# Interleaving conv blocks with the pairs of heads, respreading the adaLN steps, and fixing VectorE's order in a one-core decoder block

## The chip, the core and the metric

The kernel runs on one core of one Trainium2 chip. The metric is the device time of one execution in microseconds (us). Before the change the median of three timed runs is 1939.71 us (1936.22 to 1939.85). The core's engines each work through a queue of their own: TensorE (PE; its weight loads are shown as PEld), VectorE (DVE), ScalarE (ACT), GpSimd (POOL) and SyncE (SP), which issues the loads.

## What is computed

One decoder layer on 256 rows of 2048 columns in float32:

```
mod = silu(c) @ w_ada + b_ada                # six vectors: sh1 sc1 g1 sh2 sc2 g2
xn  = rmsnorm(x) * (1 + sc1) + sh1
q k v g | bg cg xc | gate logits = xn @ w_in
y_ret  = (rmsnorm_head(retention(rotary(q), rotary(k), v)) * silu(g)) @ w_ret_o
y_conv = (bg * conv3(cg * xc)) @ w_conv_o
h   = x + g1 * ((sig(ga) * y_ret + sig(gb) * y_conv) @ w_mix_o)
xn2 = rmsnorm(h) * (1 + sc2) + sh2
ff  = (silu(conv3(xn2 @ w_gate) + b) * (xn2 @ w_up)) @ w_down
out = rmsnorm(h + g2 * ff) * final_g
```

There are 8 heads of 256 columns, handled as four pairs; the feed-forward width is 5632.

## The kernel before

Every weight matrix is read once, in pieces of 256 rows by 512 columns (512 KB). To keep float32 accuracy a piece (`raw`) is split: ScalarE rounds it to `hi` (L304) and VectorE computes the rest, `lo = raw - hi` (L305). TensorE multiplies hi by both halves of the activations and lo by their high half. Activations are split the same way (`split`, L90).

The work is a list of **units**. A `Weights` unit is one such piece with its matmuls. `w_block` (L397) holds the weights stationary, eight units of 16 matmuls for 512 columns of output, and is used for q, k, the three conv inputs, gate and up; its four results are put together by a copy on ScalarE (L420) and an add on VectorE. `x_block` (L380) holds the activations stationary, 12 matmuls a unit, and is used for the other projections. An `Ada` unit (L310) has no matmuls of its own: it loads 128 rows of 1024 columns of w_ada and VectorE adds their product with silu(c) to an accumulator (L341). After 16 of them a sum over the partitions on TensorE gives shift or scale columns (`columns_of`, L350), or `broadcast` (L538) gives a gate's row on all partitions. `spread` (L506) puts Ada units evenly between the units of a stage.

The main loop (L1043) goes through the list: at step i it issues the load of unit i+9, prepares (hi, lo, or the adaLN step) unit i+2, runs the matmuls of unit i with what its block end (epilogue) needs, and then runs what was put off to this step by `after(n, ...)`: n steps of the list, Ada units counted. There are seven `raw` buffers and three each of `hi` and `lo`, and six PSUM banks for block results.

This is the order in which the source issues the instructions. The order on each engine is not that: the planner of the framework runs through the program with its own estimate of times and takes, engine by engine, the first instruction in source order that it holds to be ready. So an instruction that is ready early in the estimate stands earlier in the engine's queue than in the source. `tc.keep_in_program_order(ins)` puts an instruction behind the one traced just before it on its engine, without a wait for it to end; an instruction traced after it may still move ahead.

The stages by time are: a first stage in which v, the swish gate and the merge gates are computed while the first adaLN vectors arrive (to 399 us); the blocks of q and k of four pairs and the first three conv blocks (399 to 688); the retention output (688 to 785); the other nine conv blocks (785 to 999); the conv output (999 to 1096); the mixing projection (1096 to 1191); the second norm (`norm2`, L881), whose `normed` calls (L893) lie between the first feed-forward units; gate and up blocks 0 to 5 (to 1471), their down projection (to 1601), blocks 6 to 10 (to 1824) and theirs. The sequence `rotate` (L589), `scores`, `mix` and `turn` (L625 to L682) follows each k block by `after`. A conv input block ends in `gate_x` and `taps` (L740, L748). `gate_of` (L701) adds a bias that is loaded on its own and takes the sigmoid.

Of the 128 Ada units behind the first stage, 112 (`ada_mid`) are shift 2, scale 2, gate 1 and the first half of gate 2; 40 of them are spread over the q, k and first conv blocks, 13 over the retention output, 32 over the other conv blocks, 13 over the conv output and 14 over the mixing projection. The last 16 (`ada_ff`) are the second half of gate 2. The first half's broadcast is made in `norm2` (L888).

Of the kernel before, what the change touches and what calls it, by code (L numbers as in the profile page):

```python
# [10 lines left out]
F32 = mybir.dt.float32  # L11
# [4 lines left out]
ALU = mybir.AluOpType  # L16
# [3 lines left out]
D = 2048  # L20
# [3 lines left out]
CB = 512  # L24
# [13 lines left out]
ROT_AT = 24  # L38
DEFER_SG = 2
ROT_EARLY = 12  # L40
ADA_QK, ADA_RET, ADA_CONV, ADA_OUT = 40, 13, 32, 13
LAST_HEAD = 2
NORM_AHEAD = 4

# [2 lines left out]
def tile_trunk_block(  # L47
# [213 lines left out]
    later = []  # L261
    now = [0]

    def after(n, fn):
        later.append([now[0] + n, fn])

# [15 lines left out]
    class Weights:  # L282
# [11 lines left out]
        def prep(self):  # L294
            if self.in_big:
                both = blk8("hl", [P, 2, self.nk, CB], F32R)
                self.hi, self.lo = both[:, 0], both[:, 1]
            elif self.in_work:
                self.hi, self.lo = (
                    work.tile([P, self.nk, CB], F32R, tag="w4", name=nm(n)) for n in ("hw", "lw"))  # L300
            else:
                self.hi = wpool.tile([P, self.nk, CB], F32R, tag="hi", bufs=3, name=nm("hi"))
                self.lo = wpool.tile([P, self.nk, CB], F32R, tag="lo", bufs=3, name=nm("lo"))
            nc.scalar.copy(self.hi, self.raw)  # L304
            nc.vector.tensor_tensor(self.lo, self.raw, self.hi.bitcast(F32), op=ALU.subtract)  # L305

        def run(self):
            self.run_(self)
# [1 line left out]
    class Ada:  # L310
# [23 lines left out]
        def prep(self):  # L334
            acc = self.state["acc"]
            for k in range(self.nk):
                kt = self.k0 + k
                if kt == 0 and not self.bias:
                    nc.vector.tensor_scalar_mul(acc, self.raw[:, k], c_act[:, 0:1])
                    continue  # L340
                nc.vector.scalar_tensor_tensor(  # L341
                    acc, self.raw[:, k], c_act[:, kt:kt + 1], acc, op0=ALU.mult, op1=ALU.add
                )
            if self.k0 + self.nk == KT:
                self.done(acc)

# [191 lines left out]
    def broadcast(acc, store, half, name, bank):  # L538
        if "t" not in store:
            store["t"] = blk8(name, [P, D], F32)  # L540
        for s in range(2):
            ps = bank()
            nc.tensor.matmul(ps, lhsT=ones, rhs=acc[:, s, :], start=True, stop=True)
            c0 = (2 * half + s) * CB
            nc.scalar.copy(store["t"][:, c0:c0 + CB], ps)
# [2 lines left out]
        return lambda acc: broadcast(acc, g1b, half, "g1b", misc_bank)  # L548

    def gate2_done(half):  # L550
        if half:
            return lambda acc: broadcast(acc, g2b, 1, "g2b", misc_bank)
        return lambda acc: g2b.update(acc=acc)

    def vec_done(which, half):
        def done(acc):
# [7 lines left out]
    def ada_units(m, half, done, bias=False):  # L564
        st = {}
        c0 = m * D + half * 2 * CB
        return [Ada(kt, 1, c0, c0 + CB, CB, st, done, bias) for kt in range(KT)]
# [4 lines left out]
        ada_mid += ada_units(4, half, vec_done("scale", half))  # L572
    for half in range(2):
        ada_mid += ada_units(2, half, gate1_done(half), True)
    ada_mid += ada_units(5, 0, gate2_done(0), True)
    ada_ff = ada_units(5, 1, gate2_done(1), True)

    def take(extra, n):
        got = extra[:n]
# [191 lines left out]

    convs = [b for j in range(4) for b in conv_blocks(j)]

    seq = []
    for pair in range(4):
        st = retention(pair, {})
        seq += rot_block(pair * CB, st, "q")
        seq.append(decay_of(pair, st))
        seq += rot_block(D + pair * CB, st, "k")
    seq += convs[0] + convs[1] + convs[2]  # L780
    units += spread(seq, take(ada_mid, ADA_QK))

    seq = []
    for j in range(4):
# [1 line left out]
        seq += b[:2] + [gate_of(gate_a, 0, j)] + b[2:]  # L786
    units += spread(seq, take(ada_mid, ADA_RET))

    seq = [u for b in convs[3:] for u in b]
    units += spread(seq, take(ada_mid, ADA_CONV))  # L790

    mixed = []
# [88 lines left out]
    def norm2():  # L881
        ss = small.tile([P, 2], F32, tag="ss2", name="ss_h2")
        nc.vector.tensor_reduce(ss, ss_h, axis=mybir.AxisListType.X, op=ALU.add)
        r = rstd_of(ss, 2, D, "r_h")
        dr = w4("dr", [P, 2, P])
        for t in range(2):
            nc.vector.tensor_scalar_mul(dr[:, t, :], ident, r[:, t:t + 1])
        broadcast(g2b["acc"], g2b, 0, "g2b", acc_bank)  # L888
        turn_h(3)
        row["t"] = acc_bank()[:, 0:S]  # L890
        nc.tensor.matmul(row["t"], lhsT=ones, rhs=dr.rearrange("p t n -> p (t n)"), start=True, stop=True)
# [131 lines left out]
    for b0, b1_, final in ((0, cut, False), (cut, NB, True)):  # L1023
        seq = [u for j in range(b0, b1_) for u in ff_blocks(j)]
        if not final:
            seq = seq[:8] + spread(seq[8:], ada_ff, 8)
            for k0 in range(KT - 2, NORM_AHEAD - 1, -2):
                seq.insert((k0 - NORM_AHEAD) // 2 + 1, Call((lambda k: lambda: normed(k, k + 2))(k0)))
        units += seq
        if final:  # L1030
            units.append(Call(load_final))
        for j in range(4):
            args = (
                w_down, b0 * CB, j * CB,
                (lambda b: lambda kt: ff_t[b + kt // 4][:, kt % 4])(b0),
                4 * (b1_ - b0), down_epilogue(j, final),
            )
            units += last_block(*args, LAST_HEAD) if final and j == 3 else x_block(*args)


    n = len(units)
# [48 lines left out]
```

## Time and profile before

| | |
|---|---|
| median of three timed runs | 1939.71 us |
| the profiled execution | 1944.93 us |
| its span, first to last instruction | 1943.1 us |
| PE busy | 1876.3 us (97%) |
| PEld busy | 1582.6 us (81%) |
| DVE busy | 1380.0 us (71%) |
| ACT busy | 891.1 us (46%) |
| moved by DMA | 452.89 MB, mean 233 GB/s |
| mean granted TensorE clock | 0.992 |

Busy shares are means over stages with different limits. Matmuls are pipelined, so that the busy time of PE covers moments in which it starts nothing. [...] An idle time is put down to the instruction or transfer that came last.

### The profile page before, as it was taken

The page shows a single profiled execution, that of the slowest core. Times are in us where ns is not written, and L with a number is a line of the kernel's source. Part 1 is how long each engine was busy: PE and PEld are TensorE (multiplying, and loading weights), DVE is VectorE, ACT ScalarE, POOL GpSimd, SP SyncE. Part 2 cuts the span into 40 slices and gives each one's busy share as a digit, 9 for nine tenths or more (in the row PEclk, how much of TensorE's full clock was granted, in tenths as well). Part 3 has the DMA queues.
Part 4 walks back from the last instruction along what each step waited for, and adds up shares of the span by engine and source line. Part 5 has one row for each costly group of instructions (what it writes and reads, how often), then busy time and mean ns, then how long its engine had stood idle before and what let it go on. Part 6 is the DMA issues. An engine that isn't in the chain of part 4 may idle for free.

```text
span 1943.1 us, 25273 instructions
## 1 busy us (share of the span) xinstructions
PE 1876.3 (97%) x9543; PEld 1582.6 (81%) x9543; DVE 1380.0 (71%) x1638; ACT 891.1 (46%) x1150; POOL 21.8 (1%) x51
## 2 busy tenths in 40 slices
PE   5999999999999999999989999999999999999997
PEld 4788888878888877888778777888888888888886
DVE  6899987867688865677677766777765556666655
ACT  4643444534334543444444445555554335555543
POOL 1000000000000000000000000000000000000000
PEclk9999999999999999999999999999999999999999
DMA  8889986667777777787777885777665556666553
GB/s 300 305 278 308 319 306 188 207 220 242 235 234 246 237 250 245 263 269 248 249 241 259 290 266 153 232 230 225 218 205 194 192 192 192 188 192 207 193 193 112
DMA packets 222091, 452.89 MB, mean 233 GB/s; under 512 B 14932, under 2 KB 27536, under 8 KB 221584
## 3 DMA queue, kind: packets, MB, share of 16 engines
q1 hardware_dynamic: 220768, 448.99, 70.3%
q10 hardware_dynamic: 720, 2.10, 0.3%
q8 instruction: 75, 1.23, 0.2%
q14 instruction: 48, 0.39, 0.1%
q0 software_dynamic: 480, 0.18, 0.0%
HBM read 449.11 MB, written 2.10 MB: 232 GB/s over the span
## 4 chain that ended last, share of the span: by engine, by line
PE 81%; DMA 9%; DVE 6%; issue 3%; ACT 1%; SPq 0%; POOL 0%; DVEq 0%; POOLq 0%; ACTq 0%
PE acc L409 30%; PE acc L414 15%; PE acc L377 12%; PE acc L378 12%; PE acc L376 12%; DMA raw<-in_w_ada 7%; DVE lo L305 3%; DVE ada L341 1%; DMA ld<-in_b_gate 1%; PE misc L355 1%; PE misc L247 0%; ACT hi L304 0%; DMA raw<-in_w_mix_o 0%; DMA raw<-in_w_in 0%; DVE y_tok L660 0%
## 5 line engine op out<-in xcount | busy, mean ns | idle before, releaser
L304 ACT CAST hi<-raw 128x1024 fp32r<-128x1024 f32 (+1 forms) x601 | 622.9, 1038 | 837.1 <-PE acc L409 426.5
L305 DVE TENSOR_TENSOR lo<-raw,hi 128x1024 fp32r<-128x1024 f32 (+1 forms) x601 | 717.9, 1203 | 302.4 <-ACT hi L304 299.3
L409 PE MATMUL acc<-xn,hi 128*128 128x512 f32 x2688 | 852.0, 398 | 5.6 <-DVE u L734 2.5
L414 PEld LDWEIGHTS acc<-xn,lo 128*128 128x128 f32 x2688 | 507.1, 189 | 129.6 <-DVE lo L305 9.9
L414 PE MATMUL acc<-xn,lo 128*128 128x256 f32 x2688 | 531.3, 279 | 6.7 <-DVE lo L305 6.7
L409 PEld LDWEIGHTS acc<-xn,hi 128*128 128x128 f32 x2688 | 412.9, 190 | 8.8 <-DVE u L734 2.9
L341 DVE SCALAR_TENSOR_TENSOR ada<-raw,c_act,ada 128x1024 f32<-128x1024 f32 (+2 forms) x199 | 238.9, 1201 | 177.6 <-DMA raw<-in_w_ada 176.9
L377 PE MATMUL acc<-lo,ff_t 128*128 128x512 f32 x332 | 129.2, 389 | 0.0
L376 PE MATMUL acc<-hi,ff_t 128*128 128x512 f32 x332 | 129.2, 389 | 0.0
L378 PE MATMUL acc<-hi,ff_t 128*128 128x512 f32 x332 | 129.2, 389 | 0.0
L376 PE MATMUL acc<-hi,xn 128*128 128x512 f32 x304 | 119.0, 395 | 4.1 <-ACT xn L92 2.4
L377 PE MATMUL acc<-lo,xn 128*128 128x512 f32 x304 | 119.8, 394 | 1.1 <-DVE lo L305 1.1
L378 PE MATMUL acc<-hi,xn 128*128 128x512 f32 x304 | 119.4, 393 | 0.0
L420 ACT COPY sb<-acc 128x256 f32<-128x256 f32 x168 | 61.9, 370 | 44.4 <-PE acc L414 28.4
L378 PE MATMUL acc<-hw,xn 128*128 128x512 f32 x208 | 82.0, 394 | 0.0
L377 PE MATMUL acc<-lw,xn 128*128 128x512 f32 x208 | 81.9, 394 | 0.0
L376 PE MATMUL acc<-hw,xn 128*128 128x512 f32 x208 | 81.1, 394 | 0.0
L304 ACT CAST hw<-raw 128x1024 fp32r<-128x1024 f32 (+1 forms) x58 | 55.6, 959 | 48.4 <-DMA raw<-in_w_in 27.2
L377 PEld LDWEIGHTS acc<-lo,ff_t 128*128 128x128 f32 x332 | 62.3, 188 | 13.2 <-DVE lo L305 0.2
L376 PEld LDWEIGHTS acc<-hi,ff_t 128*128 128x128 f32 x332 | 62.3, 188 | 13.0
L378 PEld LDWEIGHTS acc<-hi,ff_t 128*128 128x128 f32 x332 | 62.3, 188 | 12.7
L376 PEld LDWEIGHTS acc<-hi,xn 128*128 128x128 f32 x304 | 57.1, 188 | 17.7 <-ACT xn L92 2.4
(195 smaller groups left out, 1762.4 us busy)
## 6 DMA issues: line engine op xcount, KB each, us to landing
raw<-in_w_in SPq DMA_DIRECT2D x272, 512.0 KB, 4.7
raw<-in_w_ada SPq DMA_DIRECT2D x160, 512.0 KB, 4.6
raw<-in_w_gate SPq DMA_DIRECT2D x88, 512.0 KB, 4.1
raw<-in_w_up SPq DMA_DIRECT2D x88, 512.0 KB, 4.1
raw<-in_w_down SPq DMA_DIRECT2D x88, 512.0 KB, 4.3
raw<-in_w_ret_o SPq DMA_DIRECT2D x32, 512.0 KB, 5.2
raw<-in_w_conv_o SPq DMA_DIRECT2D x32, 512.0 KB, 5.0
raw<-in_w_mix_o SPq DMA_DIRECT2D x32, 512.0 KB, 6.1
```

Source lines behind the costliest of these rows:

```text
L304: nc.scalar.copy(self.hi, self.raw)
L305: nc.vector.tensor_tensor(self.lo, self.raw, self.hi.bitcast(F32), op=ALU.subtract)
L341: nc.vector.scalar_tensor_tensor(acc, self.raw[:, k], c_act[:, kt:kt + 1], acc, op0=ALU.mult, op1=ALU.add)
L355: nc.tensor.matmul(ps[:, i:i + 1], lhsT=flat[:, (s0 + i) * P:(s0 + i + 1) * P], rhs=ones[:, 0:1], start=True, stop=True,)
L376: nc.tensor.matmul(ps, lhsT=xh, rhs=u.hi[:, k, :], start=k0 + k == first, stop=False)
L377: nc.tensor.matmul(ps, lhsT=xh, rhs=u.lo[:, k, :], start=False, stop=False)
L378: nc.tensor.matmul(ps, lhsT=xl, rhs=u.hi[:, k, :], start=False, stop=k0 + k == end - 1)
L409: nc.tensor.matmul(ps, lhsT=u.hi[:, k, i * P:(i + 1) * P], rhs=xt(k0 + k).rearrange("p h s -> p (h s)"), start=k0 + k == 0, stop=False,)
L414: nc.tensor.matmul(ps[:, 0:S], lhsT=u.lo[:, k, i * P:(i + 1) * P], rhs=xt(k0 + k)[:, 0, :], start=False, stop=last and k == UK - 1,)
L420: nc.scalar.copy(b, ps[:, S:2 * S])
```

## The change

Three things are changed. The q and k blocks of pairs 0 and 1 are followed by the three conv blocks of the first 512 columns, then come pairs 2 and 3 and the conv blocks of the next 512; six conv blocks are left for the later stage. The Ada units are respread: 6 in each pair of head pairs, 11 in each group of three conv blocks, 13 in the retention output, 24 in the six conv blocks, 12 in the conv output, and the 13 left in the mixing projection. All 32 units of gate 2 are now in the feed-forward part, 26 among the gate and up blocks and 6 in the second block of the first down projection, and both broadcasts are made where their last unit is prepared, not in `norm2`. From 12 units ahead of the first stage's end, each `lo` and each adaLN step is kept in program order on VectorE.

```diff
--- before.py
+++ after.py
@@ -38,7 +38,7 @@
 ROT_AT = 24
 DEFER_SG = 2
 ROT_EARLY = 12
-ADA_QK, ADA_RET, ADA_CONV, ADA_OUT = 40, 13, 32, 13
+ADA_QK, ADA_CONV0, ADA_RET, ADA_CONV, ADA_OUT = 6, 11, 13, 24, 12
 LAST_HEAD = 2
 NORM_AHEAD = 4
 
@@ -261,6 +261,9 @@
     later = []
     now = [0]
 
+    def in_order(ins):
+        return tc.keep_in_program_order(ins) if now[0] >= n_start else ins
+
     def after(n, fn):
         later.append([now[0] + n, fn])
 
@@ -302,7 +305,7 @@
                 self.hi = wpool.tile([P, self.nk, CB], F32R, tag="hi", bufs=3, name=nm("hi"))
                 self.lo = wpool.tile([P, self.nk, CB], F32R, tag="lo", bufs=3, name=nm("lo"))
             nc.scalar.copy(self.hi, self.raw)
-            nc.vector.tensor_tensor(self.lo, self.raw, self.hi.bitcast(F32), op=ALU.subtract)
+            in_order(nc.vector.tensor_tensor(self.lo, self.raw, self.hi.bitcast(F32), op=ALU.subtract))
 
         def run(self):
             self.run_(self)
@@ -338,9 +341,9 @@
                 if kt == 0 and not self.bias:
                     nc.vector.tensor_scalar_mul(acc, self.raw[:, k], c_act[:, 0:1])
                     continue
-                nc.vector.scalar_tensor_tensor(
+                in_order(nc.vector.scalar_tensor_tensor(
                     acc, self.raw[:, k], c_act[:, kt:kt + 1], acc, op0=ALU.mult, op1=ALU.add
-                )
+                ))
             if self.k0 + self.nk == KT:
                 self.done(acc)
 
@@ -548,9 +551,7 @@
         return lambda acc: broadcast(acc, g1b, half, "g1b", misc_bank)
 
     def gate2_done(half):
-        if half:
-            return lambda acc: broadcast(acc, g2b, 1, "g2b", misc_bank)
-        return lambda acc: g2b.update(acc=acc)
+        return lambda acc: broadcast(acc, g2b, half, "g2b", misc_bank)
 
     def vec_done(which, half):
         def done(acc):
@@ -572,8 +573,7 @@
         ada_mid += ada_units(4, half, vec_done("scale", half))
     for half in range(2):
         ada_mid += ada_units(2, half, gate1_done(half), True)
-    ada_mid += ada_units(5, 0, gate2_done(0), True)
-    ada_ff = ada_units(5, 1, gate2_done(1), True)
+    ada_ff = [u for half in range(2) for u in ada_units(5, half, gate2_done(half), True)]
 
     def take(extra, n):
         got = extra[:n]
@@ -771,14 +771,15 @@
 
     convs = [b for j in range(4) for b in conv_blocks(j)]
 
-    seq = []
-    for pair in range(4):
-        st = retention(pair, {})
-        seq += rot_block(pair * CB, st, "q")
-        seq.append(decay_of(pair, st))
-        seq += rot_block(D + pair * CB, st, "k")
-    seq += convs[0] + convs[1] + convs[2]
-    units += spread(seq, take(ada_mid, ADA_QK))
+    for half in range(2):
+        seq = []
+        for pair in (2 * half, 2 * half + 1):
+            st = retention(pair, {})
+            seq += rot_block(pair * CB, st, "q")
+            seq.append(decay_of(pair, st))
+            seq += rot_block(D + pair * CB, st, "k")
+        units += spread(seq, take(ada_mid, ADA_QK))
+        units += spread(sum(convs[3 * half:3 * half + 3], []), take(ada_mid, ADA_CONV0))
 
     seq = []
     for j in range(4):
@@ -786,7 +787,7 @@
         seq += b[:2] + [gate_of(gate_a, 0, j)] + b[2:]
     units += spread(seq, take(ada_mid, ADA_RET))
 
-    seq = [u for b in convs[3:] for u in b]
+    seq = sum(convs[6:], [])
     units += spread(seq, take(ada_mid, ADA_CONV))
 
     mixed = []
@@ -885,7 +886,6 @@
         dr = w4("dr", [P, 2, P])
         for t in range(2):
             nc.vector.tensor_scalar_mul(dr[:, t, :], ident, r[:, t:t + 1])
-        broadcast(g2b["acc"], g2b, 0, "g2b", acc_bank)
         turn_h(3)
         row["t"] = acc_bank()[:, 0:S]
         nc.tensor.matmul(row["t"], lhsT=ones, rhs=dr.rearrange("p t n -> p (t n)"), start=True, stop=True)
@@ -1023,7 +1023,7 @@
     for b0, b1_, final in ((0, cut, False), (cut, NB, True)):
         seq = [u for j in range(b0, b1_) for u in ff_blocks(j)]
         if not final:
-            seq = seq[:8] + spread(seq[8:], ada_ff, 8)
+            seq = seq[:8] + spread(seq[8:], take(ada_ff, 26))
             for k0 in range(KT - 2, NORM_AHEAD - 1, -2):
                 seq.insert((k0 - NORM_AHEAD) // 2 + 1, Call((lambda k: lambda: normed(k, k + 2))(k0)))
         units += seq
@@ -1035,7 +1035,8 @@
                 (lambda b: lambda kt: ff_t[b + kt // 4][:, kt % 4])(b0),
                 4 * (b1_ - b0), down_epilogue(j, final),
             )
-            units += last_block(*args, LAST_HEAD) if final and j == 3 else x_block(*args)
+            seq = last_block(*args, LAST_HEAD) if final and j == 3 else x_block(*args)
+            units += spread(seq, ada_ff, 4) if j == 1 and not final else seq
 
 
     n = len(units)
```

## Rows read from the trace of the kernel before

**Rows 1.** Windows: busy us and count of each engine, PE clock, DMA share, GB/s.
```profile
398.70:688.20 289.50, 280.45 (x1585) 243.55 (x1584) 220.83 (x273) 126.99 (x190) 4.11 (x5) 0.98 0.73 237
688.20:784.50 96.30, 90.36 (x402) 73.50 (x401) 60.61 (x59) 35.03 (x34) 1.66 (x3) 1.00 0.74 243
784.50:998.70 214.20, 206.47 (x1174) 177.60 (x1174) 152.11 (x171) 95.39 (x124) 3.11 (x6) 1.00 0.77 255
998.70:1096.30 97.60, 93.91 (x414) 76.24 (x413) 70.06 (x71) 38.86 (x42) 1.44 (x2) 0.98 0.76 254
1096.30:1191.40 95.10, 91.90 (x417) 75.11 (x416) 63.15 (x63) 41.45 (x52) 0.00 (x0) 1.00 0.78 261
1470.70:1601.30 130.60, 130.60 (x579) 108.14 (x577) 69.15 (x66) 51.88 (x50) 0.11 (x1) 1.00 0.57 193
1601.30:1824.20 222.90, 222.90 (x1281) 194.49 (x1280) 143.60 (x175) 115.71 (x149) 0.32 (x3) 1.00 0.61 194
```

**Rows 2.** Waits of PE, 398 to 1190 us: total us, times, longest.
```profile
PE acc L377 <- DVE lo L305: 12.5, 10, 2.1
PE acc L414 <- DVE lo L305: 6.7, 7, 1.7
PE misc L676 <- DVE y_tok L660: 4.4, 2, 2.3
...
PE misc L802 <- DVE gate_a L812: 0.2, 1, 0.2
```

**Rows 3.** Windows at and behind the first clock drop.
```profile
425.54:428.95 3.41, 3.26 (x10) 2.77 (x11) 3.38 (x6) 1.09 (x2) 0.00 (x0) 0.50 0.94 320
429.00:432.40 3.40, 3.40 (x22) 2.95 (x21) 2.10 (x3) 1.25 (x2) 0.00 (x0) 1.00 0.49 183
```

**Rows 4.** Waits of DVE, 398 to 1190 us.
```profile
DVE ada L341 <- DMA raw<-in_w_ada: 164.7, 79, 5.4
...
DVE b L362 <- PE misc L355: 3.3, 2, 2.4
```

**Rows 5.** Timeline of DVE, 414 to 426 us: start, length, idle before.
```profile
415.38 2.35 DVE L305 TENSOR_TENSOR lo<-raw,hi 128x1024 fp32r<-128x1024 f32 x2
421.75 1.28 DVE L341 SCALAR_TENSOR_TENSOR ada<-raw,c_act,ada 128x1024 f32<-128x1024 f32 x1 [4.01 <-DMA raw<-in_w_ada]
```

**Rows 6.** Timeline of SP, the same stretch.
```profile
416.63 0.34 SPq L327 DMA_DIRECT2D raw<-in_w_ada  x1
```

**Rows 7.** Timeline of DVE, 572 to 586 us.
```profile
580.30 1.29 DVE L706 TENSOR_TENSOR gate_a<-gate_a,ld 128x512 f32<-128x512 f32 x2 [3.22 <-DMA ld<-in_b_gate]
```

**Rows 8.** Timeline of PE at the second norm.
```profile
1191.44 1.88 PE L543 MATMUL acc<-ada,ones 128*128 128x512 f32 x4
...
1196.65 0.96 PE L891 MATMUL acc<-dr,ones 128*128 128x256 f32 x2 [2.10 <-DVE dr L887]
```

**Rows 9.** Groups by line on DVE, 784.5 to 998.7 us: busy, mean ns | idle before.
```profile
L305 DVE TENSOR_TENSOR lo<-raw,hi 128x1024 fp32r<-128x1024 f32 x72 | 86.2, 1218 | 2.6 <-ACT hi L304 2.6
L341 DVE SCALAR_TENSOR_TENSOR ada<-raw,c_act,ada 128x1024 f32<-128x1024 f32 x32 | 41.1, 1283 | 56.4 <-DMA raw<-in_w_ada 56.3
L751 DVE SCALAR_TENSOR_TENSOR conv<-u,vec_t,conv 128x256 f32<-128x256 f32 x12 | 5.2, 478 | 0.0
```

**Rows 10.** Groups by line on DVE, 1195 to 1215 us.
```profile
L899 DVE SCALAR_TENSOR_TENSOR u<-h_t,a,acc 128x256 f32<-128x256 f32 x14 | 6.0, 474 | 1.1 <-PE acc L891 1.1
L902 DVE SCALAR_TENSOR_TENSOR xn<-u,b,xn 128x256 fp32r<-128x256 f32 x13 | 5.6, 478 | 0.0
```

**Rows 11.** Timeline of PE, a pair's y matmuls, first and what follows the last.
```profile
522.46 0.59 PE L650 MATMUL misc<-v_tok,pt 128*128 128x256 f32 x2
...
524.86 0.58 PE L409 MATMUL acc<-xn,hi 128*128 128x512 f32 x1
```

**Rows 12.** Timeline of ACT, the last square sum of that pair.
```profile
526.10 0.19 ACT L228 ACTIVATION_READ_ACCUMULATOR junk<-misc 128x1 f32 x1
```

**Rows 13.** Timeline of DVE, that pair's y_tok.
```profile
532.17 1.66 DVE L660 SCALAR_TENSOR_TENSOR y_tok<-misc,r_y,sg_tok 128x256 f32<-128x256 f32 x4 [1.19 <-POOL r_y L222]
```

## The prediction

> **What bounds the kernel now.** I read the stages first [rows 1]: busy time of each engine, granted clock and DMA share in stretches cut where the weights change. From 1200 us on TensorE has no idle time at all: 130.60 of 130.60 in the down projection, 222.90 of 222.90 in the gate and up blocks. Those two stretches give its undisturbed pace. 1281 matmuls in 222.9 us make 2.78 us for a block unit of 16 matmuls with the weights stationary (a w unit); 579 in 130.6 us make 2.71 us for a unit of 12 with the activations stationary (an x unit). Weight loading takes 194.49/222.9 = 87.25% of the time there, and 108.14/130.6 = 82.80%.
>
> The five stages from 398.7 to 1191.4 us are slower. As a weight load costs the same everywhere, I divide each stage's weight-load time by the undisturbed share of its kind and subtract from its length: 289.5 - 243.55/0.8725 = 10.4 us lost in the q, k and first conv blocks, 96.3 - 73.50/0.828 = 7.5 in the retention output, 214.2 - 177.60/0.8725 = 10.6 in the other conv blocks, 97.6 - 76.24/0.828 = 5.5 in the conv output, 95.1 - 75.11/0.828 = 4.4 in the mixing projection: 38.4 us, all that the change could win there. [...]
>
> Next the waits of TensorE in this stretch [rows 2]: nine kinds, 29.3 us together, every one on VectorE, 19.2 us of it for low parts (`lo`). [...]
>
> Then why VectorE is late although idle a quarter of the time: its own waits [rows 4]. 164.7 us, 79 times, go to adaLN steps whose weights have not landed. The instructions around one show how [rows 5, 6]: the load is issued at 416.63, the step that reads it starts at 421.75, having held VectorE idle for 4.01 us; between them VectorE ran one low part. There are seven `raw` buffers, so in the source's order six other units would be prepared between a load and its use. The planner has pulled the step forward, and the low parts behind it, for which TensorE then waits at 424, are late.
>
> **The change part by part.** The pins put each low part and adaLN step behind the VectorE instruction traced just before it. An adaLN load then leaves when an older `raw` buffer comes free and has about five real units, 13 us and more, to land before its turn. I take all of the waits for w_ada out of this stretch, and with them TensorE's waits and clock losses, except one: at 580.30 VectorE stood 3.22 us for a b_gate load [rows 7], a gate step that the change does not pin. The y_tok wait it leads to is 2.1 of the 4.4 us in [rows 2], and the drop behind it costs 1.7. So 38.4 - 3.8 = **34.6 us go**.
>
> The respread lowers VectorE's load in the q and k blocks: 40 steps over 92 units were 40 x 1.28/92 = 0.56 us a unit, 12 over 68 are 0.23, 22 over 48 conv units 0.59, 24 over the last 48 conv units 0.64. DMA demand there is highest in the last: 72 transfers of 0.524 MB in 48 x 2.78 = 133 us are 283 GB/s, against 237 to 261 in [rows 1]; I cost it at nothing, because each load still has several units to land, and it becomes a wait only if landing takes over some 13 us. The steps' own work moves but is not changed in amount: 112 mid steps become 96 and the 16 of the second gate's first half go to the feed-forward stage, where VectorE is busy 143.60 of 222.9.
>
> What source order adds, piece by piece:
> - Gate 2's first broadcast moves from ahead of the second norm into the feed-forward stage. It took TensorE 1.88 us from 1191.44 [rows 8], some 0.15 of it the overlapped end of the last matmul. There TensorE never idles, so it costs **1.7**. At the old place the residual on VectorE and the row that TensorE waits 2.10 for still end the norm, so nothing comes back; the bounds are -0.5 (the norm's chain, freed of two copies on ScalarE) and +3.4 (1.7 more if the longer idle holds the low clock for another such stretch).
> - The start of the feed-forward stage: each unit has one low part (1.22, [rows 9]) and two normed columns of 0.474 + 0.478 [rows 10], 3.13 us against 2.78. Before, low parts were three units ahead; in source order the norm calls between the units leave one. Six units at 0.35 make **2.1**, bounds 0 and 3.5.
> - The retention chain. From the first y matmul at 522.46 to the next block's at 524.86 [rows 11] are 2.4 us; the last square sum ends at 526.29 [rows 12], 3.8 behind; then the scale, POOL (1.19 waited) and four y_tok (1.66) [rows 13]: 7.0 in all. The next pinned low part ends at 8.2, or 9.4 with an adaLN step (1.28) before it. TensorE wants it after 2.4, two units and the two leading matmuls (0.46): 8.4. Pairs 0 and 2 just fit. Pairs 1 and 3 end inside the conv blocks, where a step does fall in between: 2 x 1.0 = **2.0**, bounds 0 and 10.8 (a whole unit, 2.7, at each of four).
> - A conv input block's end. After its last matmul: copy and add about 1.0 (the nearest operation of 128x256 takes 0.478, [rows 9]), low part 1.22, gating 1.22 (the same shape), an adaLN step 1.28, four taps of 0.478, low part 1.22 make 7.8, less 0.08 overlap at each of eight borders (two low parts take 2.35 in [rows 5]): 7.2. TensorE wants that low part after two units and 0.46, at 6.0. Four blocks at 1.2 make **4.8**, bounds 0 and 11 (a unit each).
> - Shift and scale: VectorE waits for TensorE's column sums (3.3 us in two, [rows 4]), now with the next low part behind it. There is nearly a unit of slack, so **1.0** for four, bounds 0 and 9.6.
>
> Other block ends cost nothing: add and low part end some 2.2 us behind the last matmul, and TensorE has at least one unit of 2.78 or 2.71 to run. That is thin cover wherever the unit after next follows an adaLN step, and the slower rival lives there.
>
> Sum: -34.6 + 1.7 + 2.1 + 2.0 + 4.8 + 1.0 = **-23.0 us**. The profiled execution took 1944.9 us, 1943.1 of it span, so it would take 1921.9. It lies 5.2 above the median of the timed runs, 1939.7; from that median I forecast **1916.7**.
>
> **Rivals.**
> - The new waits fit into the slack. Only the broadcast is paid: -34.6 + 1.7, 1906.8. For it: low part (1.22) and share of the adaLN steps (0.23 to 0.64) take 1.5 to 1.9 us of a unit's 2.78. Against it: the two sums above that overshoot by about a microsecond.
> - The adaLN loads stay late, since the transfer and not the order is at fault: half of the waits remain, -17.3 + 11.6, 1934. For it: the landing takes 5 us and the DMA share is 0.73 to 0.78 [rows 1]. Against it: one low part between load and use [rows 5, 6].
> - Slower: strict order on VectorE. At every end of a w block a low part now stands behind adds that wait for TensorE's last matmul, and behind what the epilogue queues. If the lead there is one unit instead of two, TensorE waits about 1.2 us, as worked out for the conv input, at each of 42 such ends (8 of q and k, 12 conv, 22 feed-forward): 50 - 34.6 + 1.7 = +17.5, 1957. It decides from 0.78 us an end ((34.6 - 1.7)/42). For it: the feed-forward stage has no TensorE idle today, so the planner's free order works there. Against it: VectorE idles a third of that stage, and copy, add and low part end before one unit does. [...]
> - The order on the chip hardly changes, as later instructions were already where the source has them: 1939. [Rows 5 and 6] speak against it.
>
> **How the numbers follow.** Forecast 55%, with 1907 to 1927 of its own (new waits from half to one and a half of 11.6, the 34.6 good to about 4); new waits hidden 20%; loads still late 10%; slower 12%; no effect 3%. A measurement of this kernel tells about 0.2%, 3.9 us, from no change. Faster: 55 + 20 + 7 of the late loads = 82%; same: 3 + 3 = 6%; slower 12%. With all unknown costs at their lower ends the sum is -35.1, at their upper ends +3.7 (1905 to 1943). The range of 1900 to 1937 leaves out the slower case and some 6% below.
>
> **What would show it.** VectorE's wait for w_ada between 400 and 1190 us falls from 164.7 to under 30; TensorE's waits for `lo` there from 19.2 to under 10, with what is left right behind the conv input blocks and the retention chain; at most two clock drops instead of four; weight-load shares of the five stages near 87 and 82%; a pair of broadcast matmuls in the feed-forward stage, and small waits in its first six units. It is wrong if TensorE idles at block ends of the feed-forward stage, or if w_ada waits stay over 100 us.

## The result and the profile after

The changed kernel takes **1919.64 us** (median of 4 runs, 1919.37 to 1921.20). The kernel before took 1938.22 beside it (4 runs), so the ratio is 0.9901 with a 95% interval of 0.9885 to 0.9918: faster by 1.0%. The forecast was 1916.7, range 1900 to 1937. The medians differ by 18.6 us, where the sum had said 23.0. The profiled executions took 1944.93 before and 1921.2 after, 23.7 us less; but the one before lies 6.7 us above its median and the one after only 1.6, so the agreement with 23.0 holds for the profiles alone.

Where the stages begin (first matmul of each, us) gives the difference of the two profiles piece by piece. The q, k and conv blocks are one entry, as the change mixes them.

| stretch | before | after | change | sum said |
|---|---|---|---|---|
| up to the first q block | 398.68 | 399.58 | +0.9 | 0 |
| q, k and all conv blocks | 503.7 | 483.7 | -20.0 | } |
| retention output | 96.3 | 93.5 | -2.8 | } -26.8 |
| conv output | 97.65 | 94.5 | -3.15 | } |
| mixing projection | 95.1 | 94.55 | -0.55 | } |
| second norm | 7.92 | 6.84 | -1.1 | 0 |
| first gate and up blocks | 271.4 | 272.3 | +0.9 | +2.1 |
| first down projection | 130.6 | 132.4 | +1.8 | +1.7 |
| the rest | | | +0.3 | 0 |

The first view is that of [rows 1] for the changed kernel, with the same columns: the q and k blocks with the first half of the conv blocks, retention output, the other conv blocks, conv output, mixing, then the first gate and up blocks and the first down projection.

```profile
399.60:746.30 346.70, 343.71 (x1969) 297.49 (x1968) 257.87 (x317) 158.29 (x231) 4.16 (x6) 1.00 0.69 228
746.30:839.80 93.50, 90.93 (x402) 74.72 (x402) 62.54 (x58) 35.08 (x34) 1.43 (x2) 0.98 0.78 263
839.80:976.80 137.00, 136.28 (x786) 118.41 (x785) 105.25 (x117) 62.28 (x81) 1.73 (x5) 1.00 0.78 266
976.80:1071.30 94.50, 93.03 (x415) 74.86 (x414) 68.36 (x68) 39.04 (x42) 1.44 (x2) 1.00 0.77 262
1071.30:1165.80 94.50, 93.36 (x421) 75.69 (x419) 63.10 (x62) 42.81 (x54) 1.44 (x2) 1.00 0.76 257
1172.70:1444.90 272.20, 272.16 (x1540) 235.92 (x1541) 211.09 (x261) 143.97 (x193) 0.53 (x5) 0.99 0.73 236
1444.90:1577.30 132.40, 132.40 (x582) 108.89 (x582) 76.20 (x72) 53.03 (x52) 0.11 (x1) 1.00 0.65 215
```

Length less TensorE's busy time is 3.0 us in the first, 2.6, 0.7, 1.5 and 1.1 in the next four, and nothing in the feed-forward stage, although its low parts are pinned too. Weight loading is 85.8% and 86.4% in the two with stationary weights, 79.2 to 80.1% in the three others: nearer to the undisturbed 87.25 and 82.80, not quite there.

TensorE's waits from 398 to 1175 us, against [rows 2] (total us, times, longest):

```profile
PE acc L380 <- DVE lo L308: 4.2, 3, 2.6
PE acc L417 <- DVE lo L308: 3.3, 6, 1.2
PE misc L857 <- DVE h_tok L844: 1.9, 3, 0.9
PE acc L891 <- DVE dr L888: 1.8, 1, 1.8
PE acc L412 <- DVE xn L902: 1.8, 1, 1.8
```

VectorE's in the same stretch, against [rows 4]:

```profile
DVE lo L308 <- ACT hi L307: 111.7, 106, 3.5
DVE qk L618 <- ACT sb L423: 14.2, 22, 1.8
...
DVE ada L342 <- DMA raw<-in_w_ada: 2.0, 2, 1.2
```

The adaLN steps waited 164.7 us for their weights in one group of [rows 4]; 2.0 are left. Low parts cost TensorE 7.5 us instead of 19.2, and one clock drop is left of four. Three of the four drops of the kernel before, each with the window behind it (the other is in [rows 3]):

```profile
534.77:538.18 3.41, 3.41 (x13) 2.92 (x12) 3.41 (x7) 0.83 (x2) 0.00 (x0) 0.50 0.50 145
538.20:541.60 3.40, 3.40 (x21) 2.96 (x21) 3.37 (x4) 1.18 (x2) 0.00 (x0) 1.00 0.48 161
585.97:589.38 3.41, 3.38 (x12) 2.99 (x13) 3.41 (x5) 2.02 (x4) 0.00 (x0) 0.50 0.40 110
589.40:592.80 3.40, 3.40 (x21) 2.94 (x20) 3.40 (x8) 2.49 (x5) 0.00 (x0) 1.00 0.86 276
1012.63:1016.04 3.41, 3.41 (x10) 2.64 (x9) 1.69 (x2) 1.04 (x1) 0.00 (x0) 0.50 0.86 286
1016.10:1019.50 3.40, 3.40 (x17) 2.80 (x16) 1.51 (x3) 1.05 (x1) 0.00 (x0) 1.00 0.90 299
```

In the four drops 10 to 13 matmuls ran in 3.41 us at a granted clock of 0.50, where 17 to 22 ran in the windows behind them. A drop is costed at 1.7 us here, half its length, an estimate of mine; by these counts it is 1.3 to 1.9.

What VectorE waits for now is ScalarE's cast of the next unit, 111.7 us; as TensorE waits 7.5 us for low parts in all, most of that costs nothing.

The largest waits that are left stand where the sum had nothing. VectorE behind the last conv block of the first stage (start, length, idle before it):

```profile
747.66 0.42 DVE L759 TENSOR_TENSOR bg<-acc,sb 128x256 f32<-128x256 f32 x1 [0.99 <-ACT sb L423]
748.01 1.22 DVE L308 TENSOR_TENSOR lo<-raw,hi 128x1024 fp32r<-128x1024 f32 x1
749.14 1.22 DVE L761 TENSOR_TENSOR conv<-conv,bg 128x1024 f32<-128x1024 f32 x1
751.47 1.23 DVE L93 TENSOR_TENSOR conv_t<-conv,conv_t 128x1024 fp32r<-128x1024 f32 x1 [1.12 <-ACT conv_t L92]
752.61 1.28 DVE L344 SCALAR_TENSOR_TENSOR ada<-raw,c_act,ada 128x1024 f32<-128x1024 f32 x1
753.81 3.49 DVE L308 TENSOR_TENSOR lo<-raw,hi 128x1024 fp32r<-128x1024 f32 x3
```

TensorE there, and at the second norm:

```profile
755.08 0.79 PE L380 MATMUL acc<-lo,y_t 128*128 128x512 f32 x1 [2.57 <-DVE lo L308]
...
1166.22 0.41 PE L857 MATMUL misc<-ident,h_tok 128*128 128x128 f32 x2 [0.24 <-DVE h_tok L844]
1167.48 0.88 PE L857 MATMUL misc<-ident,h_tok 128*128 128x128 f32 x6 [0.86 <-DVE h_tok L844]
```

And the windows behind the first of these:

```profile
754.65:758.06 3.41, 2.98 (x7) 2.40 (x8) 3.41 (x4) 0.00 (x0) 0.00 (x0) 0.50 0.73 229
758.10:761.50 3.40, 3.40 (x16) 2.80 (x16) 1.62 (x2) 1.05 (x1) 0.00 (x0) 1.00 0.84 257
```

The split's subtraction (`conv_t`, L93) waits 1.12 us for ScalarE's cast. Behind it, in the source's order, stand an adaLN step and three low parts, of which two are ready by then (ScalarE's casts for them ended at 747.36 and 750.34). TensorE waits 2.57 us for the first of them, and the clock is granted at 0.50 for the next 3.41. It is the one drop that is left in these stages.

### The profile page after: what moved, and what is told of

The parts are those of the page before. It is cut to its first block, busy times and chain, and to the rows that moved or that the text cites. A ratio compares the mean times of both kernels' runs of the same rounds, so it can differ in the third digit from the quotient of the medians.

```text
span 1919.4 us, 25328 instructions
## 1 busy us (share of the span) xinstructions
PE 1873.3 (98%) x9543; PEld 1579.5 (82%) x9543; DVE 1386.4 (72%) x1638; ACT 890.5 (46%) x1150; POOL 21.7 (1%) x51
## 4 chain that ended last, share of the span: by engine, by line
PE 91%; DVE 4%; issue 2%; DMA 1%; ACT 1%; POOL 0%; SPq 0%; POOLq 0%; DVEq 0%; ACTq 0%
PE acc L412 30%; PE acc L417 15%; PE acc L380 15%; PE acc L381 14%; PE acc L379 14%; DVE lo L308 1%; PE misc L358 1%; DMA ld<-in_b_gate 1%; DMA raw<-in_w_ada 1%; PE misc L247 0%; DVE ada L344 0%; PE misc L546 0%; PE misc L632 0%; DVE conv L751 0%; ACT junk L228 0%
## 5 line engine op out<-in xcount | busy, mean ns | idle before, releaser
L412 PE MATMUL acc<-xn,hi 128*128 128x512 f32 x2688 | 840.6, 397 | 1.8 <-DVE xn L902 1.8
L417 PEld LDWEIGHTS acc<-xn,lo 128*128 128x128 f32 x2688 | 498.4, 188 | 124.2 <-DVE lo L308 10.1
L417 PE MATMUL acc<-xn,lo 128*128 128x256 f32 x2688 | 524.7, 279 | 3.6 <-DVE lo L308 3.3
L380 PE MATMUL acc<-lo,ff_t 128*128 128x512 f32 x332 | 129.3, 389 | 0.0
L380 PE MATMUL acc<-lo,xn 128*128 128x512 f32 x304 | 120.2, 395 | 1.1 <-DVE lo L308 1.1
L380 PE MATMUL acc<-lw,xn 128*128 128x512 f32 x208 | 81.8, 393 | 0.0
L380 PEld LDWEIGHTS acc<-lo,ff_t 128*128 128x128 f32 x332 | 62.3, 188 | 13.5 <-issue 0.2
```

The lines of the kernel that those rows point to most:

```text
L380: nc.tensor.matmul(ps, lhsT=xh, rhs=u.lo[:, k, :], start=False, stop=False)
L412: nc.tensor.matmul(ps, lhsT=u.hi[:, k, i * P:(i + 1) * P], rhs=xt(k0 + k).rearrange("p h s -> p (h s)"), start=k0 + k == 0, stop=False,)
L417: nc.tensor.matmul(ps[:, 0:S], lhsT=u.lo[:, k, i * P:(i + 1) * P], rhs=xt(k0 + k)[:, 0, :], start=False, stop=last and k == UK - 1,)
```

## The experiments

The theory was that the pins on the adaLN steps give the gain, by taking a wait for a DMA out of VectorE's queue, and that the new spread of the steps makes the pins cheap. Rivals were that the spread alone does it, that the pins alone do, and that the pins on low parts cost more than they give. All kernels compute the whole reference. Each ratio is to the kernel before on the same chip; waits (us) and clock drops are those of the profile between 398 and 1150 us. Runs e1 to e4 are of one chip, e5 and e7 to e9 of a second, e10 to e12 of a third; between chips the ratios are the measure, and the differences in us below are those of the medians.

| run | median us | ratio, 95% | PE waits | w_ada waits | drops |
|---|---|---|---|---|---|
| before | 1935.8 to 1938.2 | 1 | 29.2 | 169.4 | 4 |
| after | 1919.64 | 0.9901, 0.9885 to 0.9918 | 8.4 | 2.0 | 1 |
| e1 both pins, old spread | 1934.64 | 0.9993, 0.9978 to 1.0007 | 20.8 | 1.0 | 3 |
| e2 no pins, new spread | 1933.80 | 0.9990, 0.9974 to 1.0006 | 19.6 | 118.8 | 2 |
| e3 step pin, new spread | 1910.62 | 0.9855, 0.9830 to 0.9881 | 3.8 | 2.1 | 1 |
| e4 low part pin, new spread | 1939.82 | 1.0013, 0.9992 to 1.0034 | 17.4 | 104.2 | 2 |
| e5 after, cast a step ahead | 1916.01 | 0.9887, 0.9868 to 0.9906 | 6.4 | 2.0 | 0 |
| e7 step pin, old spread | 1907.07 | 0.9836, 0.9817 to 0.9854 | 1.8 | 1.3 | 1 |
| e8 e3 without interleaving | 1913.15 | 0.9867, 0.9848 to 0.9886 | 3.5 | 1.5 | 3 |
| e9 e3 with the gate adds pinned | 1906.97 | 0.9836, 0.9818 to 0.9854 | 0 | 2.5 | 1 |
| e10 e7 with the gate adds pinned | **1902.25** | 0.9825, 0.9812 to 0.9839 | 0.6 | 1.6 | 0 |
| e11 e1, low parts pinned less often | 1914.79 | 0.9886, 0.9870 to 0.9903 | 8.0 | 0.8 | 2 |
| e12 the changed kernel again | 1921.36 | 0.9922, 0.9910 to 0.9935 | 8.4 | 2.5 | 1 |

The waits of the row before are those of the one profiled execution, 1944.93 us. In e1 and e2, whose times are those of the kernel before, they are 20.8 and 19.6 us; a usual execution before probably has less than 29.2 too, but no trace of one is kept.

**e1, the pins without the spread.** The kernel before, with the two `in_order` of the diff and nothing else of it.

```diff
-            nc.vector.tensor_tensor(self.lo, ..., op=ALU.subtract)
+            in_order(nc.vector.tensor_tensor(self.lo, ..., op=ALU.subtract))
...
-                nc.vector.scalar_tensor_tensor(acc, ...)
+                in_order(nc.vector.scalar_tensor_tensor(acc, ...))
```

> The kernel before with the pins on low parts and adaLN steps alone; old sequence of blocks, old spread, both gate-2 broadcasts where they were. Theory (the order on VectorE did it): VectorE's waits for w_ada behind the first stage fall from 164.7 us to under 30 and at least half of the gain comes, but 40 steps over 92 units leave VectorE nearly full in the q and k blocks, so some low parts come late there: 1920 to 1930 us. Rival (the respread and the interleaving did it): about 1938, no faster than the kernel before.

1934.64, no change that can be told. The waits for w_ada are gone as in the changed kernel, yet nothing is gained. TensorE's waits in e1:

```profile
PE acc L417 <- DVE lo L308: 10.0, 12, 1.5
PE acc L380 <- DVE lo L308: 9.1, 4, 2.7
...
```

VectorE and then TensorE at the end of a k block in e1:

```profile
530.28 1.21 DVE L308 TENSOR_TENSOR lo<-raw,hi 128x1024 fp32r<-128x1024 f32 x1
531.41 1.22 DVE L599 TENSOR_TENSOR rot<-qk,cos_t 128x1024 f32<-128x1024 f32 x1
532.55 1.28 DVE L344 SCALAR_TENSOR_TENSOR ada<-raw,c_act,ada 128x1024 f32<-128x1024 f32 x1
533.75 1.22 DVE L601 TENSOR_TENSOR qk<-qk,sin_t 128x1024 f32<-128x1024 f32 x1
534.88 1.22 DVE L308 TENSOR_TENSOR lo<-raw,hi 128x1024 fp32r<-128x1024 f32 x1
```

```profile
531.55 1.22 PE L417 MATMUL acc<-xn,lo 128*128 128x256 f32 x8 [1.48 <-DVE lo L308]
536.15 1.21 PE L417 MATMUL acc<-xn,lo 128*128 128x256 f32 x8 [1.54 <-DVE lo L308]
```

Between two low parts VectorE does the rotation's two multiplications and an adaLN step, 1.22 + 1.28 + 1.22, and TensorE waits 1.54. So the pins exchange one kind of wait for another here, as in the slower rival: 12 waits of 0.8 us on average in the w units (L417), and four of 1.2 to 2.7 us in the x units (L380), each behind a split that waits for ScalarE. The theory had expected some late low parts in the q and k blocks, but with 1920 to 1930 us; that they would use up all of the gain it had not. The rival's time (no faster) came true without its reason, as e2 shows.

**e2, the spread without the pins.**

```diff
     def in_order(ins):
-        return tc.keep_in_program_order(ins) if now[0] >= n_start else ins
+        return ins
```

> The changed kernel without the pins: interleaving, respread and the moved broadcast alone. Theory: the planner still pulls adaLN steps ahead of low parts, w_ada waits stay over 100 us, and the time is 1930 to 1940. Rival (respread): 1918 to 1925, with TensorE's waits for low parts between 400 and 1170 us under 10 us as in the changed kernel.

1933.80, not told from no change. The wait that stays, in e2:

```profile
DVE ada L344 <- DMA raw<-in_w_ada: 114.9, 67, 5.7
```

The planner pulls the steps forward in the new spread too. The spread alone is not the gain.

**e3, only the adaLN steps pinned.** The `in_order` around `lo` is taken out of the changed kernel.

```diff
-            in_order(nc.vector.tensor_tensor(self.lo, ..., op=ALU.subtract))
+            nc.vector.tensor_tensor(self.lo, ..., op=ALU.subtract)
```

> The changed kernel with the adaLN steps pinned and the low parts free. Theory: what hurt was an adaLN step pulled forward past low parts; pinned steps alone bring w_ada waits under 30 us, and low parts that may pass a waiting subtraction remove the waits left at conv block ends: 1912 to 1920. Rival (both pins are needed, since free low parts run ahead and starve the epilogues): 1922 to 1932.

1910.62, below the theory's range and some 9 us faster than the changed kernel; the intervals of the two ratios don't meet. The pin on low parts costs.

**e4, only the low parts pinned.** The other `in_order` is taken out instead.

```diff
-                in_order(nc.vector.scalar_tensor_tensor(acc, ...))
+                nc.vector.scalar_tensor_tensor(acc, ...)
```

> The changed kernel with the low parts pinned and the adaLN steps free. Theory: the steps are still pulled ahead, w_ada waits stay over 80 us, 1926 to 1938. Rival (the low parts' order is what counts): within 0.2% of the changed kernel, 1916 to 1924.

1939.82, no gain; it lies 1.8 us above the theory's range. In e4 the steps still wait:

```profile
DVE ada L344 <- DMA raw<-in_w_ada: 99.6, 59, 4.6
```

**e5, ScalarE's cast of the conv output a step earlier,** a test of the cause read at 755 us.

```diff
-                after(2, done_b)
+                after(2, cast_b)
+                after(3, done_b)
```

(`cast_b` holds the split's copy on ScalarE, `done_b` its subtraction on VectorE.)

> The changed kernel with both pins; at a conv output-gate block's end ScalarE's cast of the product is issued two steps behind the block and VectorE's subtraction three, so that VectorE need not wait for the cast. Theory (pinned low parts stand behind a VectorE instruction that waits for ScalarE): the waits of 2.6 us at 755 and 1.4 us at 984 and the clock drop behind the first go, 1912 to 1917. Rival (the adaLN step next to it makes the low part late, not the waiting subtraction): both waits stay, 1918 to 1922.

1916.01, an interval that overlaps that of the changed kernel's first measurement and lies below that of its second (e12), so the time alone doesn't decide. In the trace the wait at 755 fell to 1.36 us and its clock drop went, and the wait at 984 went. VectorE in e5 at the first place:

```profile
750.36 1.23 DVE L772 TENSOR_TENSOR conv_t<-conv,conv_t 128x1024 fp32r<-128x1024 f32 x1 [1.12 <-ACT conv_t L768]
751.50 3.49 DVE L308 TENSOR_TENSOR lo<-raw,hi 128x1024 fp32r<-128x1024 f32 x3
```

The subtraction waits 1.12 for the cast as before. What is gone is the adaLN step (1.28) between it and the low parts: the 1.21 us won here are the rival's, and only the 1.36 that are left stand behind the waiting subtraction. At the second place no step stood between; there the subtraction now starts without a wait, with a low part ahead of it, and TensorE's wait is gone. So both causes are at work, the subtraction at both places and the step at the first.

**e7, the adaLN pin on the kernel before, nothing else.** Theory A held that the new spread is the other half of the gain, rival B that the pin alone gives it all.

```diff
-                nc.vector.scalar_tensor_tensor(acc, ...)
+                in_order(nc.vector.scalar_tensor_tensor(acc, ...))
```

> The kernel before with the adaLN steps alone pinned; its sequence and spread, low parts free. Theory A (adaLN steps pulled ahead are one half, the 40 steps over 92 units in the q and k blocks the other): w_ada waits under 30 us, the q, k and first conv stage hardly shorter than 289 us, the gain in the later stages, 1918 to 1927. Rival B (in the pins-only run the pinned low parts ate the gain, and the spread matters little): 1908 to 1914, as with the changed kernel's sequence.

1907.07, slightly below the range of rival B, which was right: the old spread is no worse than the new. TensorE's waits in e7, three kinds in 750 us:

```profile
PE acc L412 <- DVE qk L621: 0.8, 1, 0.8
PE misc L679 <- DVE y_tok L663: 0.7, 1, 0.7
PE misc L358 <- DVE ada L344: 0.3, 1, 0.3
```

Between e1 and e7 only the pin on the low parts differs: 27.6 us (the two ran on different chips, each beside the kernel before; by the ratios it is some 30). Windows of about equal length from 398 us on, first of e1 and then of e7, show it as idle time: 10.8 us without a matmul against 1.6, and 51 matmuls fewer.

```profile
398.00:686.70 288.70, 277.95 (x1585) 239.10 (x1584) 224.32 (x276) 126.27 (x191) 4.41 (x5) 1.00 0.73 240
```

```profile
398.00:686.00 288.00, 286.36 (x1636) 249.52 (x1636) 234.20 (x286) 132.74 (x196) 4.41 (x5) 1.00 0.77 249
```

**e8, e3 with all four pairs ahead of the conv blocks again.**

```diff
-        units += spread(sum(convs[3 * half:3 * half + 3], []), take(ada_mid, ADA_CONV0))
+    units += spread(sum(convs[0:3], []), take(ada_mid, ADA_CONV0))
...
-    seq = sum(convs[6:], [])
-    units += spread(seq, take(ada_mid, ADA_CONV))
+    seq = sum(convs[3:], [])
+    units += spread(seq, take(ada_mid, ADA_CONV0 + ADA_CONV))
```

> The changed kernel with low parts free and adaLN steps pinned, and without the interleaving: all four pairs, three conv blocks, then the retention output and nine conv blocks; the adaLN steps respread (12 in the pairs, 11 in the first three conv blocks, 35 in the nine). Theory: it is the number of steps beside the q and k blocks that counts, not the sequence of blocks: 1908 to 1914. Rival (the conv blocks between the pairs matter by themselves): 1916 to 1924.

1913.15, an interval that overlaps that of e3. Mixing conv blocks with the pairs is not needed, as long as low parts are free.

**e9 and e10, the gate bias adds pinned as well,** on e3 and on e7.

```diff
-                nc.vector.tensor_tensor(g, g, got.t, op=ALU.add)
+                in_order(nc.vector.tensor_tensor(g, g, got.t, op=ALU.add))
```

> The changed kernel with low parts free, adaLN steps pinned and the gate bias additions pinned too, which VectorE executes some 100 us ahead of their place in the source and then waits 7.8 us for their loads. Theory: these waits go and with them the last early-step stalls and the clock drop at 729: 1904 to 1909. Rival (the waits lie in VectorE's slack): within 0.2% of the kernel without that pin, 1908 to 1913.

> The kernel before with the adaLN steps and the gate bias additions pinned, low parts free, its sequence and spread. Theory: the last waits for b_gate loads go as they did in the changed sequence, 1904 to 1907, the fastest of all. Rival (those 2.1 us of waits lie in VectorE's slack here): within 0.2% of the run with the adaLN pin alone, 1905 to 1910.

1906.97 and 1902.25: 3.7 and 4.8 us less than without, but on other chips; by the ratios 3.7 and 2.1, with intervals that overlap, so the size is not firm and a gain is not shown. In e3 gate adds waited 9.0 us for `in_b_gate` (7.8 of them `gate_a`), one more instruction that waits for a DMA and was pulled ahead; in e9 and e10 none waits. e9 lies in its theory's range, but the clock drop that was to go with the waits is still there, from 722.5. e10, below both its ranges, has the lowest median of all, 1.75% below the kernel before by its ratio. What TensorE still waits for in 750 us of e10:

```profile
PE misc L358 <- DVE ada L344: 0.6, 1, 0.6
```

**e11, what in the low parts' pin costs.** e1, but a low part is pinned only where the instruction traced just before it on VectorE is another low part or an adaLN step; behind epilogue instructions the planner stays free.

```diff
+    def behind_preps(ins):
+        before = next(i for i in reversed(nc.cur_bb.bb.instructions)
+                      if i is not ins.ins and i.engine == ins.ins.engine)
+        preps.add(ins.ins.name)
+        return in_order(ins) if before.name in preps else ins
...
-            in_order(nc.vector.tensor_tensor(self.lo, ..., op=ALU.subtract))
+            behind_preps(nc.vector.tensor_tensor(self.lo, ..., op=ALU.subtract))
```

> The pins-only kernel (old sequence and spread, adaLN steps pinned) with a low part pinned only where the VectorE instruction traced just before it is another low part or an adaLN step, not where it is an epilogue's. Theory (a pinned low part is late because it stands behind an epilogue instruction that waits for TensorE, ScalarE or POOL): 1905 to 1913. Rival (low parts in source order are late wherever they stand, since VectorE is nearly full in the q and k blocks): 1928 to 1938, as with all low parts pinned.

1914.79: 20 of the 27.6 us come back, slightly less than the theory's range asked for. The rest is looked for in e11's trace. VectorE, then TensorE:

```profile
680.28 1.23 DVE L93 TENSOR_TENSOR conv_t<-conv,conv_t 128x1024 fp32r<-128x1024 f32 x1 [1.98 <-ACT conv_t L92]
681.42 1.28 DVE L352 SCALAR_TENSOR_TENSOR ada<-raw,c_act,ada 128x1024 f32<-128x1024 f32 x1
682.62 3.49 DVE L316 TENSOR_TENSOR lo<-raw,hi 128x1024 fp32r<-128x1024 f32 x3
```

```profile
683.89 0.50 PE L388 MATMUL acc<-lo,y_t 128*128 128x512 f32 x1 [2.51 <-DVE lo L316]
```

The low part is pinned behind an adaLN step, and that step is itself pinned behind the split. This costs two waits of 2.51 us; in two more, of 1.20 and 1.21, the step stands behind `y_tok`, which waits 1.19 for POOL, and behind the split of `mixed`, which waits 2.30 for ScalarE. Against e7 TensorE waits 6.2 us more (8.0 to 1.8) and has one more clock drop of 1.7, together 7.9, about the 7.7 that are missing. That these places are all of the rest was read from the trace, not tried.

**e12, the changed kernel once more,** beside e10 and e11.

> The changed kernel once more, beside the others on one chip: 1917 to 1922, 9 to 15 us above the kernel before with the adaLN pin alone.

1921.36, with the waits of the first profile again. On one chip e10 and the changed kernel differ by 19 us.

## Why the prediction was right, and where its steps were not

**The mechanism was right, and the runs show it.** A step that waits for its DMA was pulled forward on VectorE, low parts stood behind it, and TensorE waited. Pinning that one instruction (e7) takes 169.4 us of waits to 1.3 and is worth 1.6%; leaving it free (e2, e4) leaves over 100 us of waits and no gain. The fourth rival, that the order hardly changes, falls with it, and so does "loads stay late": from 400 to 1150 us a load of w_ada takes 4.7 us by the median from issue to landing both before and in e7, so the transfer is as slow as it was, and in the source's order it has time to land.

**The size was right in the profiles, by errors that cancel, and too large for the medians.** In the five stages the sum had 34.6 - 2.0 - 4.8 - 1.0 = 26.8 us less; they lost 26.5. But both sides of that sum were too small. From the first q block to the end of the mixing projection, in the kernel before and in e10 (3985 and 3986 matmuls in the traces):

```profile
398.68:1191.44 792.76, 763.15 (x3985) 646.01 (x3984) 566.81 (x634) 337.72 (x441) 10.31 (x16) 0.99 0.75 248
```

```profile
400.11:1150.59 750.48, 749.88 (x3986) 641.69 (x3985) 572.42 (x635) 338.29 (x441) 10.32 (x16) 1.00 0.80 263
```

e10 is 42.3 us shorter, where the prediction had 38.4 as all that there was to win. The step that failed is "a weight load costs the same everywhere", an assumption of mine that no run shows: in [rows 3] eleven loads take 2.77 us at a clock of 0.50 and 21 take 2.95 at 1.00 (0.25 and 0.14 us a load), so the time of the loads, which was divided, held a part of the loss (646.01 against 641.69). The changed kernel needs 766.22 us here, 15.7 more than e10, where the sum left 38.4 - 26.8 = 11.6. That 3.9 too little on one side met 4.1 too little on the other is luck. Of the 15.7, time without a matmul (8.9 against 0.6) and the clock drop (1.7) are 10.0; where the other 5.7 lie is open.

One more step of the forecast was off: the loss was read from an execution 5.2 us above the median and subtracted in full from the median. The medians fell by 18.6 us, and by 14.5 on the chip of e12. How much of the surplus was loss that a usual execution does not have is open, for want of a trace of one.

The terms:

- *The gate event that stays, 3.8.* Of this, 1.7 was half of the drop's 3.41 us, which no run shows as such: from 585.97 on 12 matmuls ran in it, and 21 in the window behind. The gate add at 645.88 ran without a wait; two waits of TensorE behind it are 0.60 and 0.40, and `y_tok` of a pair stands just ahead, so even these are not surely its own. Mis-sized by at least 2.8. Four other gate adds wait 4.2 us for their loads, with no wait of TensorE right behind them; in e3 these adds wait 9.0 us.
- *Conv input block ends, 4 x 1.2.* Three are seen, at 554.07, 895.10 and 964.56, of 0.41, 0.36 and 0.36. The place was right and the price three times too high. The chain of 7.2 us had an adaLN step (1.28) in it at every end; without one the chain would be 5.9, under the 6.0 that TensorE leaves. Which of its links is shorter was not tried.
- *Retention chain, 2 x 1.0.* Pair 3 waited 1.19 at 697.02, behind an adaLN step and two low parts as described; pair 1 did not.
- *Shift and scale, 1.0.* Nothing is seen.
- *"Other block ends cost nothing."* This step failed. The blocks that end a conv gate cost 2.57 and 1.37 us and a clock drop of 1.7, 5.6 together. I had costed copy, add and low part, and left out the split behind them: a subtraction on VectorE that waits 1.1 us for a cast on ScalarE, to which the next low part is now tied, at the first place with an adaLN step (1.28) between.
- *The broadcast, +1.7* was 1.8. *The norm, 0* was -1.1: the matmuls that were moved away (1.88, [rows 8]) had covered only part of the residual's path, so TensorE now waits 0.24 and 0.86 for `h_tok`, and the rest came back. It lies inside the bounds of -0.5 and +3.4 for the pair of terms (+1.8 - 1.1 = +0.7). The 1.7 in the upper bound, for one more stretch of low clock, is shown by no run: the clock behind the norm stood at 0.50 for 6.83 us before (from 1196.95) and for 6.83 after (from 1171.08).
- *The start of the feed-forward stage, 2.1* is 0.9 for the stage, and no wait of TensorE is seen in it: low parts and norm columns alternate on VectorE as described, but it keeps up, and even waits 2.98 us for ScalarE at 1182.18. Some 0.4 of the 0.9 is the low clock behind the norm (0.62 against 0.68 over the first 6.8 us); the rest stays open.

**What the prediction did not weigh was which pin does it.** It took pins and spread as one, and put the slower rival at 12% as an alternative. That rival was in part at work inside the result. In the old spread the pins on low parts cost 27.6 us (e1 against e7) and use up the whole gain. The rival gave about 1.2 us an end; e1 shows 0.8 in each of twelve waits in w units, and 9.1 us in four waits behind splits, which the rival did not have. Its count was too large, as the feed-forward stage, 22 of its 42 ends, shows none. In the new spread the same pins cost some 9 us (after against e3), probably because fewer adaLN steps fall among the rotations; no run varies that number alone. So the respread, which I credited with a lower load on VectorE, shows no worth of its own (e7 against e3, e8): together with the interleaving it pays back 15 us (e1 against after) of a cost that the change itself brings.

On both sides of this change VectorE kept low parts that were ready standing behind an instruction that waited: before, behind a DMA wait of 4.01 us that ended at 421.75 [rows 5], when ScalarE's cast for the next low part had ended at 420.10; after, two behind a cast wait of 1.12 us.

## What to carry to other kernels

Where ready work stands behind an instruction that waits, as on VectorE here (4.01 us before, 1.12 after), pin the instructions that wait for a DMA and nothing needs soon, and leave those free that another engine waits for: e10 does that with two pins and is 1.75% faster, while pinning both kinds in the same spread gave nothing. Before costing a pin, write down everything that its block's end puts on the engine up to the last instruction, with the waits for other engines in it, and not only the first two. And try each part of such a change alone: two of the parts here worked against each other, and the sum hid it. A loss that is read from one profile belongs to that execution: see where its time lies among the others before subtracting it from their median.

## What was not expected of the hardware

In four kernels the clock fell with next to no idle time of TensorE. In e7 the sixteen one-column matmuls of a column sum take 1.99 us with 0.30 of waiting ahead of them; the matmul behind takes 0.78 us. TensorE, and then the windows ahead of it and from 723.39 on, in e7:

```profile
721.62 1.99 PE L358 MATMUL misc<-ones,ada 128*128 128x1 f32 x16 [0.30 <-DVE ada L344]
723.47 0.78 PE L380 MATMUL acc<-lo,y_t 128*128 128x512 f32 x1
```

```profile
718.00:721.00 3.00, 3.00 (x15) 2.43 (x13) 3.00 (x5) 1.06 (x1) 0.00 (x0) 1.00 0.90 288
723.39:726.80 3.41, 3.41 (x10) 2.73 (x10) 1.18 (x2) 1.04 (x1) 1.65 (x3) 0.50 0.83 282
726.80:730.20 3.40, 3.40 (x17) 2.81 (x16) 0.83 (x2) 1.05 (x1) 0.00 (x0) 1.00 0.57 173
```

e9 has the same without any wait of TensorE before 1150 us: sixteen such matmuls in 1.95 us from 719.89, and 0.50 from 722.5 on. In e3 and e8 such sums take 1.98 and 1.95 us after 0.44 and 0.33 of waiting, and the drops follow at 728.8 and 730.9. Not every such sum brings it; e10 has the same four and no drop before 1150 us. In the changed kernel, waits of 1.19 and 1.37 us left the clock alone (1.00 in the 3.41 us from 697.02 and from 984.30 on) and 2.57 did not (0.50 from 754.65 on).
